# The order of the expert steps and the last scatter of a mixture-of-experts kernel

## The chip, the core and the metric

The kernel runs on one core of a Trainium2 chip. The core has a matmul engine (TensorE, PE in the profile; its weight loads are listed apart as PEld), a vector engine (VectorE, DVE), an engine for activations (ScalarE, ACT), a general one (GpSimd, POOL) and one that issues transfers (SyncE, SP), each with its own queue of instructions, and 16 DMA engines that move data between HBM and the on-chip memory. The metric is the device time of one execution in microseconds (us), the median of several; lower is better.

## The reference

Two layers of a diffusion backbone over 256 latent tokens and 256 context tokens with width 1024. Each layer mixes tokens by two kinds of gated recurrences and then channels; the first layer's channel mix is a dense SwiGLU, the second one's a mixture of eight experts, and only the latent tokens go through it. The change is about that last part and the final norm:

```python
logits = (t @ router).astype(jnp.float32)
top_v, top_i = lax.top_k(logits, TOP_K)                 # two of eight experts for each of 256 tokens
top_w = jax.nn.softmax(top_v, axis=-1)
gates = jnp.sum(jax.nn.one_hot(top_i, N_EXPERTS) * top_w[..., None], axis=1)
for e in range(N_EXPERTS):                              # w1, w3: 1024 x 3584, w2: 3584 x 1024, all float32
    y = y + gates[:, e:e + 1] * ((jax.nn.silu(t @ w1[e]) * (t @ w3[e])) @ w2[e])
x = x + m_lat[5] * y
return rmsnorm(x, final_norm_g)
```

## The kernel before, in words

Up to about 1000 us the kernel computes everything ahead of the experts; the change does not touch that. Then it routes the tokens: it counts how many go to each expert and sorts experts 1 to 7 by their count, so that from there on "expert r" is a rank (rank 0 is always expert 0). The ranks 1 to 4 have room for 128 tokens (`BIG`), the ranks 0, 5, 6 and 7 for 64 (`SMALL`); where an expert has more tokens than its room, code at the end of the kernel goes over them again, which the profiled execution did not enter.

The weights of an expert come as 42 tiles of 1 MB, and its work is cut into seven steps. A step (r, c) takes 512 columns of the hidden width: four tiles of w1 and w3 for the up product, two tiles of w2 for the down product. `steps` (line 182 on) lists the 56 steps of all experts in the order in which they run, the 128-slot ones in one sequence, the 64-slot ones in another, and `due` says how many of the 64-slot ones have to be placed by each position. The loop at line 1236 runs one turn for each step: the up product of step n (`up_big`, `up_small`), then the down product of step n-1 (`lower`), then the transposes of step n's hidden values (`turn_big`, `turn_small`), whose copy the down product of the next turn reads.

A 128-slot step computes in three products of two float32r halves: each half tile of weights is split into a high part by ScalarE (`wh`) and a low part by VectorE (`wl`), and TensorE multiplies wh by the tokens' high part, wl by the high part, and wh by the low part. A 64-slot step multiplies the float32 tiles as they are, two halves of the array side by side, and needs no split. The up product goes into the PSUM tiles `pj`, the down product of a 128-slot expert accumulates over its seven steps in two `po` tiles, that of a 64-slot expert in one `pj` tile, with rows 0 to 63 for the first 512 output columns and rows 64 to 127 for the others.

Three things sit beside the products. Before an expert's first step its tokens are gathered: `open_group` makes the one-hot matrix, `gather_group` multiplies by it in four pieces (with ScalarE and VectorE copying the results out), `back_group` transposes it for the way back. Two experts may share a gather (`members`): a 128-slot one and a 64-slot one. After an expert's last step `close` weighs the sum with the modulation, and `scatter` splits it (`halves`) and spreads it back over the tokens (`spill`: two matmuls and one VectorE sum into `x2t` for each half of the columns and each half of the tokens). For a 128-slot expert this is one scatter for each half of the columns, in two successive turns; for a 64-slot one a single scatter. `rest` hands gathers and scatters to `lower`, which puts one of them behind every group of down matmuls. After the last step `finish_half` squares and sums the residual for one half of the columns and multiplies by the norm's gain, and `finish_out` scales and writes.

The order of the instructions on each engine is the order of the code here (`strict[0]`), so an instruction waits for all those ahead of it on its engine. SyncE's queue issues the tiles in the order of `plan`: the up tiles of step n, then the down tiles of step n-1. A tile goes into the next of 12 buffers, and its transfer is issued when the buffer is free: for a 64-slot step when TensorE has used it, for a 128-slot step when both of its halves are split. `taken_pieces` (line 1173) sets how far the issue and the splits run ahead of the product: up to six half tiles, but no more than three that are split.

Of the kernel before, what the change touches and what calls it, by code (L numbers as in the profile page):

```python
# [16 lines left out]
D, T, KT = 1024, 256, 8  # L17
W, R = 64, 4
NE, DE = 8, 3584
# [15 lines left out]
def body(ctx, tc, I, out, dbg=None):  # L35
    nc = tc.nc
# [145 lines left out]
    big = [(r, c) for r in BIG for c in range(7)]  # L182
    small = [(r, c) for r in SMALL for c in range(7)]
    steps = []
    total, lead, tail = len(small), 3, 4
    for i in range(7 * NE):
        due = i + 1 if i < lead else min(total, lead + (i + 1 - lead) * (total - lead) / (7 * NE - lead - tail))
        steps.append((small if total - len(small) < int(due) else big).pop(0))
    chosen = {}

# [733 lines left out]
    def onehot(pos, widths):  # L924
        P = sb(mp, [128, 2, 256], F32R, "P", 1)
        o = 0
        for i, w in enumerate(widths):
            iota = C_IOTA if w == 128 else C_IOTH
            DVE.tensor_tensor(P[:, :, o:o + 128], con[:, None, iota:iota + 128].to_broadcast([128, 2, 128]),
                              pos[i].to_broadcast([128, 2, 128]), op=ALU.is_equal)  # L930
            o += 128
        return P
# [11 lines left out]
    def big_tiles():  # L944
        return sb(mp, [128, KT, 128], F32R, "xgh", 2), sb(mp, [128, KT, 128], F32R, "xgl", 2)

    def small_tile():
        return sb(mp, [128, KT, 64], F32, "xgs", 2)
# [135 lines left out]
    def down_big(ws, c, aT, ys, mid=(), halfway=None):  # L1084
        mid = list(mid)
        order = [(f, i) for f in range(4) for i in range(2)]
        if halfway:
            order[5:7] = order[6:4:-1]
        for n, (f, i) in enumerate(order):
            wt = tuple(t[:, 512 * i:512 * i + 512] for t in ws(f))  # L1090
            mm3(ys[i], (aT[0][:, f], aT[1][:, f]), wt, c == 0 and f == 0, c == 6 and f == 3)
            if mid:
                mid.pop(0)()
            if halfway and n == 5:
                halfway()
        for f in mid:
            f()
# [36 lines left out]
        return lambda tt: gater[:, tt, r:r + 1]  # L1134

    def members(g):
        return [g] + ([g + 4] if 0 < g < 4 else [])

    def open_group(g):
        if len(members(g)) == 2:  # L1140
            hot[g] = onehot([posr[:, :, g:g + 1], posr[:, :, g + 4:g + 5]], [128, 64])
            xgs[g], xgs[g + 4] = big_tiles(), small_tile()
        else:
            hot[g] = onehot([posr[:, :, g:g + 1]], [128])
            xgs[g] = big_tiles()

    def gather_group(g, k):
        gather([xgs[r] for r in members(g)], k, hot[g])
# [24 lines left out]
    def taken_pieces(n):  # L1173
        first = taken[0]
        taken[0] += n

        def at(k):
            i = first + k
            while (len(emitted) <= i or len(emitted) <= i + LOOK and sum(len(x) == 2 for x in emitted[i + 1:]) < 3) \
                    and next(feeder, 0) is None:  # L1180
                pass
            return tuple(x[:, 0] for x in emitted[i])
        return at
# [3 lines left out]
    def at_step(table, n, f):  # L1187
        table.setdefault(n, []).append(f)
# [6 lines left out]
        at_step(after, 0, lambda h=h: ACT.activation(m5[:, 512 * h:512 * h + 512], rows5[h], AF.Copy))  # L1195
    n = -5
    for g in BIG:
        free = {2: (0,), 3: (1, 5), 4: (2,)}.get(g, ())
        n = max([n + 5] + [1 + steps.index((r, 6)) for r in free])
        assert all(n + (3 if g == 1 else 4) <= steps.index((r, 0)) for r in members(g)), (g, n)  # L1200
        at_step(early if n else before, n, lambda g=g: open_group(g))
        for k in range(0, KT, 2):
            at_step(mids, n + 1 + k // 4 if g == 1 else n + k // 2, lambda g=g, k=k: gather_group(g, k))
        at_step(mids, n + 4, lambda g=g: back_group(g))
    acc, jobs = {}, []

    def close_half(r, i):
        jobs.append((r, weigh(acc[r][i], [(every, i)]), [(every, i)]))
# [8 lines left out]
    def scatter():  # L1217
        if not jobs:
            return []
        r, t, cuts = jobs.pop(0)  # L1220
        y = halves(t)
        return [lambda rows=rows, i=i, tt=tt: spill(y, rows, back[r], gate_of(r), i, tt)
                for rows, i in cuts for tt in range(2)]

    def lower(r, c, aT, mid):
        if c == 0:
            acc[r] = [bank("po") for i in range(2)] if r in BIG else bank("pj")
        if r in BIG:
            down_big(taken_pieces(4), c, aT, acc[r], mid)
        else:  # L1230
            down_small(taken_pieces(4), c, aT, acc[r], mid)
        if c == 6:
            close(r)
# [19 lines left out]
    r, c, aT = prev  # L1253
    z = sb(raws, [128, 2, D], F32, "w")

    left = []

    def begin(i):
        if i == 0:
            tc.keep_in_program_order(nc.scalar.preload_act_table_set("abs_reciprocal_sqrt_and_small"))  # L1260
        close_half(r, i)
        left.extend(scatter())

    down_big(taken_pieces(4), c, aT, acc[r], (), lambda: begin(0))
    for i in range(2):
        while left:
            left.pop(0)()
        if i == 0:
            begin(1)
        finish_half(z, i)  # L1270
    finish_out(z)
    strict[0] = False
# [133 lines left out]
```

## Time and profile before

| | before |
|---|---|
| median of 3 runs | 1889.72 us (1889.15 to 1893.68) |
| profiled execution | 1886.93 us, of which the span of the program 1885.1 us |
| TensorE busy | 1825.1 us (97%) |
| VectorE busy | 1203.9 us (64%) |
| ScalarE busy | 947.7 us (50%) |
| moved by DMA | 495.1 MB, mean 263 GB/s |
| expert weights | 336 transfers of 1 MB |
| TensorE's granted clock, mean | 0.99 |

Times in the profile are in us from the first instruction. Every matmul, split and copy of this kernel is recorded with line 47, that of a helper, so the rows are told apart by the names of the tiles: `pj<-w,xgs` is an up matmul of a 64-slot step, `pj<-w,aT` a down matmul of one (each listed as two instructions), `pj<-wh,xgh` and its like an up matmul of a 128-slot step, `po<-wh,aTh` a down matmul of one, `pp<-con,a` the transposes, `pp<-P,htkh` a gather, `pp<-y,PTa` or `PTb` a scatter. The end of a matmul is modelled, so that of two successive ones the starts tell more than the durations. An idle time in brackets names what ended it.

### The profile page before, as it was taken

What the parts mean: (1) busy time and instruction counts of PE and PEld (TensorE: products, weight loads), DVE (VectorE), ACT (ScalarE), POOL (GpSimd) and SP (SyncE); (2) the same over time, 40 slices, a digit from 0 to 9 for tenths busy, and PEclk for the clock granted to TensorE, in tenths of its full rate; (3) what the DMA queues carried; (4) which work ended last, traced back from release to release, by engine and by line L of the source; (5) the groups of instructions that cost most, each with busy time, mean ns of one, the idle gap of its engine ahead of it and who ended that gap; (6) DMA issues with size and microseconds to landing.
All of it is one profiled execution on the core that took longest, in us unless ns stands there. A gap on an engine that the chain in (4) does not pass through costs nothing.

```text
span 1885.1 us, 30248 instructions
## 1 busy us (share of the span) xinstructions
PE 1825.1 (97%) x11901; PEld 1329.5 (71%) x11901; DVE 1203.9 (64%) x1923; ACT 947.7 (50%) x1506; POOL 49.4 (3%) x94
## 2 busy tenths in 40 slices
PE   6999999999999999999999999999999999999995
PEld 4887778988888888987884556565656566565574
DVE  5699985788875337566763556565565656566485
ACT  4757664532222235666663545454455545354464
POOL 0111010000000000110000000000000000000000
PEclk9999999999999999999999999999999999999998
DMA  9344212456774324311264999999999999999991
GB/s 359 110 161 136 90 47 90 157 201 216 262 268 148 106 79 140 110 50 68 78 255 186 421 422 421 421 422 421 421 420 421 421 421 421 421 420 422 421 412 41
DMA packets 76731, 495.10 MB, mean 263 GB/s; under 512 B 8448, under 2 KB 10752, under 8 KB 23072
## 3 DMA queue, kind: packets, MB, share of 16 engines
q1 hardware_dynamic: 76576, 493.03, 66.1%
q8 instruction: 97, 1.59, 0.4%
q14 instruction: 58, 0.48, 0.1%
HBM read 491.95 MB, written 1.05 MB: 262 GB/s over the span
## 4 chain that ended last, share of the span: by engine, by line
PE 77%; DMA 8%; DVE 6%; ACT 6%; issue 2%; SPq 0%; ACTq 0%; DVEq 0%
PE pj L47 61%; PE po L47 11%; DMA w<-in_mw 7%; PE pp L47 6%; DVE wl L47 1%; ACT wh L47 1%; ACT kpad L47 1%; DVE junk L47 1%; DMA wm<-in_wmod 1%; ACT ptd L47 1%; DMA xT<-in_xT 1%; DVE Q L47 0%; DVE nt L47 0%; ACT F L47 0%; DVE hl L47 0%
## 5 line engine op out<-in xcount | busy, mean ns | idle before, releaser
L47 DVE TENSOR_TENSOR wl<-w,wh 128x1024 fp32r<-128x1024 f32 (+1 forms) x501 | 598.5, 1214 | 225.2 <-ACT wh L47 213.0
L47 ACT ACTIVATE wh<-w 128x1024 fp32r<-128x1024 f32 (+1 forms) x501 | 518.0, 1048 | 347.0 <-PE pj L47 260.5
L47 PE MATMUL pj<-hh,wh 128*128 128x512 f32 (+1 forms) x992 | 349.3, 353 | 1.5 <-ACT hh L47 1.0
L47 PE MATMUL pj<-hh,wl 128*128 128x512 f32 (+1 forms) x992 | 347.8, 351 | 1.7 <-DVE wl L47 1.7
L47 PE MATMUL pj<-hl,wh 128*128 128x512 f32 (+1 forms) x992 | 348.7, 352 | 0.5 <-DVE hl L47 0.5
L47 PEld LDWEIGHTS pj<-hh,wh 128*128 128x128 f32 x992 | 186.5, 188 | 30.3 <-issue 3.4
L47 PEld LDWEIGHTS pj<-hl,wh 128*128 128x128 f32 x992 | 186.7, 188 | 27.6 <-issue 2.5
L47 PEld LDWEIGHTS pj<-hh,wl 128*128 128x128 f32 x992 | 186.6, 188 | 26.6 <-DVE wl L47 2.5
L47 PE MATMUL pj<-w,xgs 128*64 128x512 f32 x896 | 199.8, 599 | 0.0
L47 DVE SCALAR_TENSOR_TENSOR junk<-wm,cbc 128x1024 bf16<-128x1024 f32 x128 | 156.3, 1221 | 41.3 <-DMA wm<-in_wmod 39.8
L47 PE MATMUL pj<-wh,xgh 128*128 128x512 f32 x448 | 180.5, 403 | 0.0
L47 PE MATMUL pj<-wl,xgh 128*128 128x512 f32 x448 | 178.5, 399 | 0.2 <-DVE wl L47 0.2
L47 PE MATMUL pj<-wh,xgl 128*128 128x512 f32 x448 | 178.1, 398 | 0.0
L47 PEld LDWEIGHTS pj<-w,xgs 128*64 128x64 f32 x896 | 62.2, 138 | 117.6 <-issue 116.9
L47 ACT ACTIVATE a<-pj 128x256 f32<-128x256 f32 (+1 forms) x78 | 40.3, 517 | 187.6 <-PE pj L47 187.6
L47 DVE TENSOR_TENSOR a<-a,pj 128x256 f32<-128x256 f32 (+1 forms) x78 | 45.9, 590 | 137.7 <-PE pj L47 85.0
L47 PE MATMUL pj<-w,aT 128*64 128x512 f32 x448 | 106.2, 602 | 0.0
L47 PEld LDWEIGHTS pj<-wl,xgh 128*128 128x128 f32 x448 | 84.8, 189 | 20.6 <-DVE wl L47 1.4
L47 PEld LDWEIGHTS pj<-wh,xgl 128*128 128x128 f32 x448 | 84.8, 189 | 20.5
L47 PEld LDWEIGHTS pj<-wh,xgh 128*128 128x128 f32 x448 | 84.8, 189 | 19.3
L47 PE MATMUL po<-wh,aTh 128*128 128x512 f32 x224 | 94.1, 420 | 0.7 <-ACT aTh L47 0.7
L47 PE MATMUL po<-wl,aTh 128*128 128x512 f32 x224 | 89.8, 401 | 0.9 <-DVE wl L47 0.9
(273 smaller groups left out, 2442.1 us busy)
## 6 DMA issues: line engine op xcount, KB each, us to landing
w<-in_mw SPq DMA_DIRECT2D x336, 1024.0 KB, 18.5
wm<-in_wmod SPq DMA_DIRECT2D x80, 512.0 KB, 4.1
w<-in_win SPq DMA_DIRECT2D x31, 1024.0 KB, 4.8
w<-in_fw SPq DMA_DIRECT2D x30, 1024.0 KB, 4.9
w<-in_wout SPq DMA_DIRECT2D x12, 1024.0 KB, 4.8
wg<-in_wgroup SPq DMA_DIRECT2D x8, 1024.0 KB, 14.2
w<-in_fw SPq DMA_DIRECT2D x8, 768.0 KB, 4.3
xT<-in_ctxT SPq DMA_DIRECT2D x1, 1024.0 KB, 8.0
```

Of the source, the lines that this page charges most:

```text
L47: ins = fn(*args, **kw)
```

## The change

It has three parts. The list of steps begins with four 64-slot steps instead of three and ends with three 64-slot steps behind the spread-out part instead of four steps of 128 slots; with B for a 128-slot step and s for a 64-slot one the two orders are

```
before  sssBsBsBsBsBsBsBsBsBsBsBsBsBsBsBsBsBsBsBsBsBsBsBsBssBBBB
now     ssssBBsBsBsBBsBsBsBBsBsBsBBsBsBsBBsBsBsBBsBsBsBBsBsBssss
```

Since the 64-slot experts come later, rank 7 shares its gather with rank 4 instead of rank 3, and the pieces of a gather are placed by the turn in which the group is first needed. And because the last step is now of a 64-slot expert, the last scatter is one split with four spreads, with `finish_half` for a half of the columns behind the two spreads that complete it; the code that closed the first half of a 128-slot expert in the middle of its last down product is no longer called.

```diff
--- before.py
+++ after.py
@@ -182,9 +182,10 @@
     big = [(r, c) for r in BIG for c in range(7)]
     small = [(r, c) for r in SMALL for c in range(7)]
     steps = []
-    total, lead, tail = len(small), 3, 4
+    total, lead, tail = len(small), 4, 3
     for i in range(7 * NE):
-        due = i + 1 if i < lead else min(total, lead + (i + 1 - lead) * (total - lead) / (7 * NE - lead - tail))
+        mid = (i + 1 - lead) * (total - lead - tail) / (7 * NE - lead - tail)
+        due = i + 1 if i < lead else lead + mid if i < 7 * NE - tail else total - (7 * NE - 1 - i)
         steps.append((small if total - len(small) < int(due) else big).pop(0))
     chosen = {}
 
@@ -1134,12 +1135,13 @@
         return lambda tt: gater[:, tt, r:r + 1]
 
     def members(g):
-        return [g] + ([g + 4] if 0 < g < 4 else [])
+        return [g] + {1: [5], 2: [6], 4: [7]}.get(g, [])
 
     def open_group(g):
         if len(members(g)) == 2:
-            hot[g] = onehot([posr[:, :, g:g + 1], posr[:, :, g + 4:g + 5]], [128, 64])
-            xgs[g], xgs[g + 4] = big_tiles(), small_tile()
+            o = members(g)[1]
+            hot[g] = onehot([posr[:, :, g:g + 1], posr[:, :, o:o + 1]], [128, 64])
+            xgs[g], xgs[o] = big_tiles(), small_tile()
         else:
             hot[g] = onehot([posr[:, :, g:g + 1]], [128])
             xgs[g] = big_tiles()
@@ -1195,12 +1197,15 @@
         at_step(after, 0, lambda h=h: ACT.activation(m5[:, 512 * h:512 * h + 512], rows5[h], AF.Copy))
     n = -5
     for g in BIG:
-        free = {2: (0,), 3: (1, 5), 4: (2,)}.get(g, ())
+        free = {2: (0,), 3: (1,), 4: (2, 5)}.get(g, ())
         n = max([n + 5] + [1 + steps.index((r, 6)) for r in free])
-        assert all(n + (3 if g == 1 else 4) <= steps.index((r, 0)) for r in members(g)), (g, n)
+        first = min(steps.index((r, 0)) for r in members(g))
+        per = 2 if n + 4 <= first and g > 1 else 4
+        done = (n + 1 if g == 1 else n) + KT // per
+        assert done <= first, (g, n)
         at_step(early if n else before, n, lambda g=g: open_group(g))
         for k in range(0, KT, 2):
-            at_step(mids, n + 1 + k // 4 if g == 1 else n + k // 2, lambda g=g, k=k: gather_group(g, k))
+            at_step(mids, done - KT // per + k // per, lambda g=g, k=k: gather_group(g, k))
         at_step(mids, n + 4, lambda g=g: back_group(g))
     acc, jobs = {}, []
 
@@ -1253,20 +1258,12 @@
     r, c, aT = prev
     z = sb(raws, [128, 2, D], F32, "w")
 
-    left = []
-
-    def begin(i):
-        if i == 0:
-            tc.keep_in_program_order(nc.scalar.preload_act_table_set("abs_reciprocal_sqrt_and_small"))
-        close_half(r, i)
-        left.extend(scatter())
-
-    down_big(taken_pieces(4), c, aT, acc[r], (), lambda: begin(0))
+    tc.keep_in_program_order(nc.scalar.preload_act_table_set("abs_reciprocal_sqrt_and_small"))
+    lower(r, c, aT, ())
+    left = scatter()
     for i in range(2):
-        while left:
-            left.pop(0)()
-        if i == 0:
-            begin(1)
+        for f in left[2 * i:2 * i + 2]:
+            f()
         finish_half(z, i)
     finish_out(z)
     strict[0] = False
```

VectorE ahead of the first 128-slot step, before (`wl` is the low part of a weight split, `a` the hidden values of a step, `xgl` the low part of gathered tokens; the numbers are those of buffers, which differ between the two programs):

```order
L47 TENSOR_TENSOR a_10510<-a_10510,pj_10485 128x256
L47 TENSOR_TENSOR xgl_10471<-g_10527,xgh_10470 128x256
L47 TENSOR_TENSOR xgl_10471<-g_10545,xgh_10470 128x256
L47 TENSOR_TENSOR wl_10585<-w_10582,wh_10584 128x1024
L47 TENSOR_TENSOR wl_10591<-w_10582,wh_10590 128x1024
L47 TENSOR_TENSOR a_10596<-a_10596,pj_10563 128x256
L47 TENSOR_TENSOR wl_10602<-w_10599,wh_10601 128x1024
L47 TENSOR_TENSOR xgl_10471<-g_10616,xgh_10470 128x256
L47 TENSOR_TENSOR xgl_10471<-g_10634,xgh_10470 128x256
L47 TENSOR_TENSOR wl_10653<-w_10599,wh_10652 128x1024
```

The same place now:

```order
L47 TENSOR_TENSOR a_10510<-a_10510,pj_10485 128x256
L47 TENSOR_TENSOR xgl_10471<-g_10527,xgh_10470 128x256
L47 TENSOR_TENSOR xgl_10471<-g_10545,xgh_10470 128x256
L47 TENSOR_TENSOR a_10588<-a_10588,pj_10563 128x256
L47 TENSOR_TENSOR xgl_10471<-g_10604,xgh_10470 128x256
L47 TENSOR_TENSOR xgl_10471<-g_10622,xgh_10470 128x256
L47 TENSOR_TENSOR wl_10662<-w_10659,wh_10661 128x1024
L47 TENSOR_TENSOR wl_10668<-w_10659,wh_10667 128x1024
L47 TENSOR_TENSOR a_10673<-a_10673,pj_10640 128x256
L47 TENSOR_TENSOR wl_10679<-w_10676,wh_10678 128x1024
```

The product `a` of the step ahead of the first 128-slot one stands behind two splits as before, one step later in the plan; the last two gather copies, which stood behind three splits, now have none ahead of them.

VectorE at the end of the program, before, from the last split on (`a<-po` weighs, `y` is the low part of the scatter's split, `x2t` the sums of the scatter, `w<-x2t` the product with the norm's gain, `fr` the sum of squares):

```order
L47 TENSOR_TENSOR wl_16256<-w_16233,wh_16255 128x1024
L47 TENSOR_TENSOR a_16278<-po_15192,m_9881 128x512
L47 TENSOR_TENSOR y_16280<-a_16278,y_16280 128x512
L47 SCALAR_TENSOR_TENSOR x2t<-pp_16289,gater,x2t 128x512
L47 SCALAR_TENSOR_TENSOR x2t<-pp_16293,gater,x2t 128x512
L47 TENSOR_TENSOR a_16297<-po_15193,m_9881 128x512
L47 TENSOR_TENSOR y_16299<-a_16297,y_16299 128x512
L47 TENSOR_TENSOR w_16254<-x2t,xgh_15546 128x512 x2
L47 SCALAR_TENSOR_TENSOR x2t<-pp_16308,gater,x2t 128x512
L47 SCALAR_TENSOR_TENSOR x2t<-pp_16312,gater,x2t 128x512
L47 TENSOR_TENSOR w_16254<-x2t,xgh_15546 128x512 x2
L47 TENSOR_TENSOR fr<-fs 128x2
```

And now, from the weighing of the last expert on:

```order
L47 TENSOR_TENSOR a_16260<-a_16260,pj_16235 128x256
L47 TENSOR_TENSOR a_16288<-pj_15498,m_9881 64x512 x2
L47 TENSOR_TENSOR y_16291<-a_16288,y_16291 128x512
L47 SCALAR_TENSOR_TENSOR x2t<-pp_16294,gater,x2t 128x512
L47 SCALAR_TENSOR_TENSOR x2t<-pp_16298,gater,x2t 128x512
L47 TENSOR_TENSOR w_16278<-x2t,xgh_15849 128x512 x2
L47 SCALAR_TENSOR_TENSOR x2t<-pp_16308,gater,x2t 128x512
L47 SCALAR_TENSOR_TENSOR x2t<-pp_16312,gater,x2t 128x512
L47 TENSOR_TENSOR w_16278<-x2t,xgh_15849 128x512 x2
L47 TENSOR_TENSOR fr<-fs 128x2
```

The two weighings are of 64 rows each and stand together, with one split for both halves of the columns; the sums and products behind them are in the same order as before.

TensorE at the end, before, from the last down matmuls on:

```order
L47 MATMUL po_15193<-wh_16235,aTl_16251 128x512
L47 MATMUL po_15193<-wh_16255,aTh_16250 128x512
L47 MATMUL po_15193<-wl_16256,aTh_16250 128x512
L47 MATMUL po_15193<-wh_16255,aTl_16251 128x512
L47 MATMUL pp_16289<-y_16280,PTa_14007 128x512 x2
L47 MATMUL pp_16293<-y_16280,PTa_14007 128x512 x2
L47 MATMUL pp_16308<-y_16299,PTa_14007 128x512 x2
L47 MATMUL pp_16312<-y_16299,PTa_14007 128x512 x2
```

And now:

```order
L47 MATMUL pp_16273<-con,a_16260 128x128 x2
L47 MATMUL pj_15498<-w_16254,aT_16276 64x512 x4
L47 MATMUL pj_15498<-w_16263,aT_16276 64x512 x4
L47 MATMUL pp_16294<-y_16291,PTb_14013 128x512 x2
L47 MATMUL pp_16298<-y_16291,PTb_14013 128x512 x2
L47 MATMUL pp_16308<-y_16291,PTb_14013 128x512 x2
L47 MATMUL pp_16312<-y_16291,PTb_14013 128x512 x2
```

The last down product is eight matmuls of a 64-slot step, and the four spreads follow it without a weighing between them.

## Rows read from the trace of the kernel before

**Rows 1.** The page's part 2: what the DMA engines moved in 40 slices.
```profile
GB/s 359 110 161 136 90 47 90 157 201 216 262 268 148 106 79 140 110 50 68 78 255 186 421 422 421 421 422 421 421 420 421 421 421 421 421 420 422 421 412 41
```

**Rows 2.** What SyncE's queue waited for, 1036 to 1140 us: total, times, longest.
```profile
SPq L47 <- DMA w<-in_mw: 82.5, 41, 2.1
```

**Rows 3.** The same, 1500 to 1780 us.
```profile
SPq L47 <- PE pj L47: 93.4, 51, 5.8
...
SPq L47 <- DMA w<-in_mw: 46.4, 33, 2.4
```

**Rows 4.** Timeline: start, length, engine, operation; TensorE at starts of steps, two of ScalarE.
```profile
1182.74 1.51 PE L47 MATMUL pj<-w,xgs 128*64 128x512 f32 x6
...
1190.17 1.06 ACT L47 ACTIVATE wh<-w 128x1024 fp32r<-128x1024 f32 x1 [0.49 <-DMA w<-in_mw]
...
1203.90 0.48 PE L47 MATMUL pj<-wh,xgh 128*128 128x512 f32 x1
...
1220.70 0.65 PE L47 MATMUL pj<-w,xgs 128*64 128x512 f32 x2
...
1263.66 0.47 PE L47 MATMUL pj<-wh,xgh 128*128 128x512 f32 x1
...
1280.94 0.65 PE L47 MATMUL pj<-w,xgs 128*64 128x512 f32 x2
...
1610.72 0.65 PE L47 MATMUL pj<-w,xgs 128*64 128x512 f32 x2
...
1627.00 0.48 PE L47 MATMUL pj<-wh,xgh 128*128 128x512 f32 x1
...
1642.59 0.65 PE L47 MATMUL pj<-w,xgs 128*64 128x512 f32 x2
...
1655.47 0.47 PE L47 MATMUL pj<-wh,xgh 128*128 128x512 f32 x1
...
1671.06 0.65 PE L47 MATMUL pj<-w,xgs 128*64 128x512 f32 x2
...
1772.12 0.65 PE L47 MATMUL pj<-w,xgs 128*64 128x512 f32 x2
...
1784.01 0.44 PE L47 MATMUL pp<-con,a 128*128 128x128 f32 x2 [1.38 <-DVE a L47]
...
1784.55 0.39 ACT L47 ACTIVATE aT<-pp 128x256 f32<-128x256 f32 x1 [0.83 <-PE pp L47]
...
1838.12 0.48 PE L47 MATMUL pj<-wh,xgh 128*128 128x512 f32 x1
```

**Rows 5.** Windows: length, busy PE, PEld, DVE, ACT, POOL, clock, DMA share, GB/s.
```profile
1655.47:1671.06 15.59, 15.59 (x72) 10.42 (x70) 7.70 (x7) 6.18 (x7) 0.00 (x0) 1.00 1.02 421
1820.80:1838.12 17.32, 17.32 (x80) 13.96 (x78) 15.71 (x15) 13.49 (x14) 0.00 (x0) 1.00 0.95 396
```

**Rows 6.** Windows, after the last tile.
```profile
1842.00:1844.00 2.00, 2.00 (x10) 1.63 (x9) 1.81 (x3) 1.33 (x2) 0.00 (x0) 1.00 0.00 0
```

**Rows 7.** Timeline: a 64-slot down product, the last down matmul, the sum of squares.
```profile
1061.48 3.65 PE L47 MATMUL pj<-w,aT 128*64 128x512 f32 x16
...
1862.11 0.39 PE L47 MATMUL po<-wh,aTl 128*128 128x512 f32 x1
...
1871.20 0.15 DVE L47 TENSOR_TENSOR fr<-fs 128x2 f32<-128x2 f32 x1
```

**Rows 8.** Timeline ahead of the first 128-slot step.
```profile
1043.42 2.00 ACT L47 ACTIVATE wh<-w 128x1024 fp32r<-128x1024 f32 x2 [11.34 <-DMA w<-in_mw]
...
1046.79 0.41 DVE L47 TENSOR_TENSOR a<-a,pj 128x256 f32<-128x256 f32 x1
...
1048.35 0.44 PE L47 MATMUL pp<-con,a 128*128 128x128 f32 x2 [3.69 <-DVE wl L47]
```

**Rows 9.** Windows with a lower clock.
```profile
1048.50:1052.00 3.50, 3.50 (x11) 2.73 (x11) 0.85 (x2) 2.94 (x9) 0.00 (x0) 0.53 1.01 421
1195.50:1202.00 6.50, 6.50 (x19) 4.62 (x20) 3.45 (x4) 1.77 (x4) 0.00 (x0) 0.50 1.01 416
```

## The prediction, made before the changed kernel ran

> **What bounds the kernel now.** I read the page's slices first, then who waits for whom, then the order of time around the first and the last expert steps, since the change touches nothing ahead of 1018 us. From there to the last two the slices stand at 420 to 422 GB/s [rows 1], which looks like a kernel that waits for its weights. The queue that issues the transfers says otherwise. Early in the expert stage SyncE waits for earlier transfers, 82.5 us of 104 [rows 2]; between 1500 and 1780 us it waits for them only 46.4 us of 280, and 93.4 us for a tile that TensorE has yet to free [rows 3]. The transfers run ahead, and TensorE holds their buffers.
>
> TensorE's own rows bear this out. A cycle is the time from one step's first matmul to the next one's: the up product of the new step, the down product of the step before, the transposes between. A 64-slot up behind a 128-slot step costs 12.88 us (1642.59 to 1655.47), a 128-slot up behind a 64-slot step 15.59 (1655.47 to 1671.06), two 64-slot steps 10.51 up to the next transposes (1772.12 to 1784.01, less the 1.38 of waiting) [rows 4]. Two 128-slot steps in a row cost 17.32, the stretch from the first matmul of the last step but one to that of the last, in which TensorE is busy throughout [rows 5]. A step's six tiles of 1.049 MB need 6 x 2.49 = 14.94 us at 421 GB/s. An alternating pair takes TensorE 28.47 us and the transfers 29.88; what TensorE has to do besides (gathers, scatters) fills the difference and more. Both are nearly full, TensorE slightly fuller: no tile lands after 1842 us [rows 6], and TensorE's last down matmul ends at 1862.50 [rows 7], 20 us later.
>
> The Trainium skill ("Perfetto Trace Analysis", section "Identifying the Most-Contended Engine") would have TensorE's headroom judged by its weight loads and the transfers by HBM utilization; by that page's table of peaks 421 GB/s is 118% of a core's share, while the weight loads fill 67% of an alternating cycle here [rows 5], so by the rule the transfers bind and the first rival's time below would come out. The trace disagrees in the later part, where the issuing queue waits for buffers [rows 3].
>
> **The change, part by part.** First, the start. Before the first 128-slot step TensorE waits 3.69 us for the transposes at 1048.35: the product they need stands on VectorE behind two weight splits, and these wait for a tile that lands at 1043.42 and for the one 2.49 later [rows 8]. With a fourth small step in front, the tiles of the first 128-slot step come six tiles, 14.94 us, later in the plan: 1058.4 and 1060.9. The two ScalarE splits behind the first take until 1060.5, VectorE's until 1061.9, the product 0.41: the transposes come free at about 1062.3. In the rows of before they come 1.15 us after the product ends, behind gather evacuations caught in the same queue; in the new order no split stands ahead of these, so I leave this out, and keep 1063.3 as the upper end. After its wait TensorE ran at a granted clock of 0.53 for 3.5 us [rows 9]; this is inside the sum of before, and I let it stand once in the new one.
>
> Second, the middle. From 1048.35 to the last step's first matmul at 1838.12 [rows 4, 8] are 789.8 us in 52 cycles: 25 of a 128-slot up behind a 64-slot step, 24 the other way, two of two large, one of two small, 389.8 + 309.1 + 34.6 + 10.5 = 744.0 us; the other 45.8 are gathers, scatters, stalls. The new order has 51 cycles there: 21, 21, seven, two, or 327.4 + 270.5 + 121.2 + 21.0 = 740.1 us. Of the 45.8 two items go. The cycle at 1182.74 takes 21.16 us, 8.28 over its price, though its parts are a 64-slot scatter (3.40: 1610.72 to 1627.00 is 16.28 against 12.88) and one gather (1.21: 1203.90 to 1220.70 is 16.80 against 15.59): 3.7 us are a pile-up, in which ScalarE waits for a tile at 1190.17 [rows 4] and TensorE runs at half clock for 6.5 us [rows 9]. In the new order this scatter and this gather fall on two 128-slot steps in a row, and the tiles next in the plan are a 64-slot step's, which have no split to block VectorE's queue; I let the 3.7 go. The other is the 1.38 us ahead of the transposes at 1784.01, where TensorE had caught up with the transfers. The last expert's scatter leaves this stretch and that of expert 4 enters it: 3.40 out, two halves of 1.69 in (1263.66 to 1280.94 is 17.28 against 15.59 [rows 4]), nothing in sum. That leaves 40.7. The last step starts at 1062.3 + 740.1 + 40.7 = 1843.1, 5.0 us later than before.
>
> Third, the end. Before, from the last step's first matmul to the end of its last down matmul are 1862.50 - 1838.12 = 24.4 us. Now a 64-slot up and down follow: 10.5 to the transposes, 0.9 to the end of the copy behind them (1784.01 to 1784.94 [rows 4]), 3.65 for the down product [rows 7], 15.1 us: 1858.2, that is 4.3 us earlier. The tiles are there by then. The first of the four closing steps starts 12.9 + 2 x 10.5 + 2 x 1.7 us ahead of the last one, at 1806; at full rate its first tile lands 25 tiles before the last, at 1842 - 62 = 1780, so all twelve buffers are held. Of the 26 tiles from it on, 14 to 16 have yet to land, 40 us at the most, and TensorE needs 52 for them.
>
> Fourth, the last scatter. Behind the last down matmul VectorE had, in order, `y`, two sums, `a`, `y`, two products, two sums, two products: 11 instructions, and the end of the chain at 1871.20, 8.7 us after [rows 7]. Now it has two `a`, one `y` and the same eight: 11 again, each on 512 columns. One wait for ScalarE goes, and the first half's sums are no longer begun under the down product's end. I take nothing in sum, 0.7 us either way. The activation table is loaded under the last down product, where ScalarE has nothing else.
>
> The sum is 4.3 us less on the profiled execution of 1886.9 us: 1882.6. The median of the runs shown is 2.8 above that execution: 1885.4. About 5.7 us (0.3%) is the least that a measurement of this kernel tells from no change. The unknown costs: the start 1.0 later, or 1.5 earlier without the half clock; the rest of the stalls inside the 40.7 gone, some 2 less; one more pile-up, 3.7 more. That is 1882 to 1890 for this case.
>
> **Rivals.** *The transfers are the bound.* Then the end follows the last tile: 1842 us and 1.8 for the half of the down product that it feeds, 1843.8 in place of 1862.5, 18.7 less: 1871. For it: 421 GB/s in every slice, and TensorE's waits at both ends of the stage stem from tiles [rows 4, 8]. Against it: the 740 us of prices are TensorE's work without a wait in it, and a new order sheds none of it. This is the gain that shows if the end is looked at alone.
>
> *Pile-ups of scatter and gather.* The new order brings the two together in six cycles (12, 16, 17, 28, 29 and 30, counted from 0); before it was four (12, 26, 31, 32), and one of them cost 3.7 us beyond its parts. One of the six has large steps on both sides, where VectorE is busy 15.71 of 17.32 us without them [rows 5]. From the third that pays, the result is over the bound: -4.3 + 3 x 3.7 = +6.8; with four, +10.5: 1900. Against it: the other three of before paid nothing, with TensorE further behind the transfers, as it will be here.
>
> *The start costs what the end gives.* If the later first large step brings a second stretch at half clock (another 1.5) and the upper end of its wait (1.0), and one pile-up stays (3.7), the sum is +1.9: 1892. Every part of that is seen in before.
>
> **How the numbers follow.** The forecast's case gets 0.65, the transfers 0.07, pile-ups from three on 0.12, the start with one pile-up 0.16. The forecast's spread of 1882 to 1890 has the bound of 1884.05 inside its lower third, so 0.26 of its 0.65 is faster; with the transfers' case 0.33. Slower are the pile-ups, 0.12. The rest, 0.55, is no change that can be measured. The range of 1880 to 1894 leaves out the transfers' case, most of the pile-ups and a little on the low side.
>
> **What would show it.** The transposes ahead of the first 128-slot step at 1062 to 1063.5 us; the last step's first matmul at 1840 to 1846; the end of its last down matmul some 15 us later; then 8.7 us to the end of the chain. The transfers should fall below 421 GB/s somewhere in the last 150 us before the closing steps, because TensorE holds all twelve buffers; before, they did so only at the end. The cycle of the first scatter should take 17.3 + 4.6 us and no more. I am wrong on the main point if TensorE waits for tiles in the last four steps, or if its cycles no longer come at these prices.

## The result, and the profile after

The changed kernel takes 1881.31 us (median of 5 runs, 1878.13 to 1883.87), the kernel before 1889.72 beside it: a ratio of 0.995, with a 95% interval of 0.9933 to 0.9967. It is faster by 0.5%, beyond the 0.3% that a measurement tells from no change. The forecast was 1885.4 us, 4.3 us off the path; the path lost more.

To compare executions I count from the first matmul of the expert stage, because that stage began at anything from 1006.92 to 1014.18 us in the 13 profiles of this study, although the change touches nothing ahead of it. In the profile of before it is at 1008.33 us and the last down matmul ends at 1862.49, 854.16 later; after, 1010.61 and 1858.43, 847.82 later. That is 6.34 us less. Then 8.46 us to the sum of squares where it was 8.70.

The first view is the page's slices of GB/s, 40 of them, which answer to [rows 1].

```profile
GB/s 360 104 164 128 102 47 89 158 190 222 238 268 178 90 94 141 91 69 68 68 231 185 421 421 421 421 421 421 421 421 420 396 400 419 421 420 414 405 422 153
```

From slice 32 on the transfers fall to 396 and 400, again to 405 near the end: every buffer is taken, and a transfer waits until one comes free. What SyncE's queue waited for between 1500 and 1780 us says the same (total, times, longest), against [rows 3]:

```profile
SPq L47 <- DVE wl L47: 121.2, 54, 4.9
SPq L47 <- PE pj L47: 95.7, 45, 5.4
SPq L47 <- DVE a L47: 1.9, 6, 0.3
```

The 46.4 us of waiting for earlier transfers are gone; every wait is for a buffer. And TensorE, from its first 128-slot step to the last transposes, shows no wait for another engine at all.

The timeline (start, length, engine, operation, idle time before it) ahead of the first 128-slot step, where [rows 8] had the transposes at 1048.35 with 3.69 us of waiting:

```profile
1053.46 1.94 PE L47 MATMUL pj<-w,xgs 128*64 128x512 f32 x8 [0.53 <-DMA w<-in_mw]
1056.04 1.94 PE L47 MATMUL pj<-w,aT 128*64 128x512 f32 x8 [0.64 <-DMA w<-in_mw]
1058.43 1.94 PE L47 MATMUL pj<-w,aT 128*64 128x512 f32 x8 [0.46 <-DMA w<-in_mw]
1064.74 0.69 PE L47 MATMUL pp<-con,a 128*128 128x128 f32 x2 [4.36 <-DVE a L47]
```

The turn of the fourth 64-slot step itself waits for three tiles, and the long wait stands where it stood, one step later. The last step and the tail, against the end of [rows 4] and [rows 7]:

```profile
1843.35 3.22 PE L47 MATMUL pj<-w,xgs 128*64 128x512 f32 x14
...
1854.78 3.65 PE L47 MATMUL pj<-w,aT 128*64 128x512 f32 x16 [0.53 <-ACT aT L47]
1858.48 1.39 DVE L47 TENSOR_TENSOR a<-pj,m 64x512 f32<-64x512 f32 x2 [7.15 <-PE pj L47]
...
1861.85 1.41 DVE L47 SCALAR_TENSOR_TENSOR x2t<-pp,gater,x2t 128x512 f32<-128x512 f32 x2 [0.59 <-PE pp L47]
...
1863.17 1.29 DVE L47 TENSOR_TENSOR w<-x2t,xgh 128x512 f32<-128x512 f32 x2
...
1864.37 1.41 DVE L47 SCALAR_TENSOR_TENSOR x2t<-pp,gater,x2t 128x512 f32<-128x512 f32 x2
...
1865.69 1.28 DVE L47 TENSOR_TENSOR w<-x2t,xgh 128x512 f32<-128x512 f32 x2
...
1866.89 0.16 DVE L47 TENSOR_TENSOR fr<-fs 128x2 f32<-128x2 f32 x1
```

15.08 us from the last step's start to the end of its down product, where before had 24.4; behind it VectorE's instructions follow each other without a gap from 1861.85. Three windows of this kernel (length, busy PE, PEld, DVE, ACT, POOL, clock, DMA share, GB/s): the cycle of the first scatter, which shares its turn with a gather, the stretch behind the wait at the start, and two us behind the last tile.

```profile
1186.42:1208.19 21.77, 21.77 (x95) 15.71 (x94) 16.77 (x19) 12.41 (x17) 0.00 (x0) 1.00 1.01 420
...
1064.75:1068.25 3.50, 3.50 (x10) 2.87 (x11) 2.29 (x2) 1.56 (x3) 0.00 (x0) 0.56 1.01 419
1851.50:1853.50 2.00, 2.00 (x12) 0.57 (x8) 0.00 (x0) 0.00 (x0) 0.00 (x0) 1.00 0.00 0
```

The scatter's cycle is TensorE's work alone, at full clock. The half clock at the start stands once, as before. The last tile is there by 1851.5, though TensorE's last product that needs it begins only at 1854.78 and reaches it 5.2 us after it landed.

### The profile page after: what moved, and what is told of

The parts are those of the page before. It is cut to its first block, busy times and chain, and to the rows that moved or that the text cites. A ratio compares the mean times of both kernels' runs of the same rounds, so it can differ in the third digit from the quotient of the medians.

```text
span 1881.9 us, 30271 instructions
## 1 busy us (share of the span) xinstructions
PE 1821.9 (97%) x11901; PEld 1330.4 (71%) x11901; DVE 1206.6 (64%) x1923; ACT 947.1 (50%) x1506; POOL 49.4 (3%) x94
## 5 line engine op out<-in xcount | busy, mean ns | idle before, releaser
L47 DVE TENSOR_TENSOR a<-a,pj 128x512 f32<-128x512 f32 (+1 forms) x78 | 46.0, 590 | 135.4 <-ACT a L47 80.3
L47 ACT ACTIVATE a<-pj 128x512 f32<-128x512 f32 (+1 forms) x78 | 40.2, 516 | 178.3 <-PE pj L47 178.2
L47 PE MATMUL po<-wh,aTl 128*128 128x512 f32 x224 | 88.8, 396 | 0.0
## 6 DMA issues: line engine op xcount, KB each, us to landing
w<-in_mw SPq DMA_DIRECT2D x336, 1024.0 KB, 12.8
```

What stands on the lines that cost most here:

```text
L47: ins = fn(*args, **kw)
```

## The experiments

All device times below are medians beside runs of before on the same chip; "the path" is the time from the first expert matmul to the end of the last down matmul in the profiled execution.

**What sets the end, before and after.** In the next two kernels the second w2 tile of the steps 20 to 35 is not loaded; the first is used in its place, so the products are the same in number and the values are not. 16 transfers of 2.49 us, 40 us, are left out. The edit is the same in the changed kernel and in the one before:

```diff
+    last = [None]
...
-        w = chunk(src() if callable(src) else src, a, b)
+        if src == "again":
+            w = last[0]
+        else:
+            w = last[0] = chunk(src() if callable(src) else src, a, b)
...
+            if 20 <= i - 1 < 36:
+                plan[-1] = ("again",) + plan[-1][1:]
```

In the changed kernel:

> The changed kernel with the second tile of the down weights left out in steps 20 to 35: the step uses its first tile twice, so 16 of 336 transfers (40 us at 2.49) are not made, with all splits and matmuls as they were. If TensorE sets the time from the first 128-slot step to the end, nothing moves: 847.8 us from the first expert matmul to the last down matmul's end, within 1 us. If the transfers set it, up to 40 us less.

Measured: 1881.82 us, path 847.73 against 847.82. The tiles do not set the changed kernel's time; since TensorE waits for no engine from the first 128-slot step on, its own work does.

In the kernel before:

> The kernel before with the same 16 transfers left out. By TensorE's ledger only the waits at 1782 to 1784 us go, 1.5 us: 852.7 us from the first expert matmul to the last down matmul's end in place of 854.2. If the transfers set the time up to the four closing steps, up to 40 us less.

Measured: 1882.76 us, a ratio to before of 0.9968 (0.9954 to 0.9982), path 849.46: 4.7 us less than before. That is three times what I had expected from TensorE's work and a tenth of what the transfers' rival wanted. SyncE's queue between 1500 and 1780 us, against [rows 3], and the window where [rows 9] had a clock of 0.50 (the stage began 1.75 us later):

```profile
SPq L47 <- PE pj L47: 111.9, 57, 7.5
SPq L47 <- DVE wl L47: 105.7, 46, 4.9
```

```profile
1197.20:1203.70 6.50, 6.50 (x33) 4.84 (x32) 4.35 (x7) 3.97 (x9) 0.00 (x0) 1.00 1.01 413
```

With the tiles early, the waits for transfers go, and so does the wait of [rows 4] at 1784; the stretch at half clock is not there either, although the kernel is the same as before up to this point. That leaves a doubt: 2.95 of the 4.7 us lie in the cycle of that stretch and 0.7 at the start, ahead of the first tile left out. The cycle took 21.16 us in before and takes 18.21 here:

```profile
1184.64:1202.85 18.21, 17.32 (x75) 8.67 (x75) 12.56 (x16) 9.69 (x15) 0.00 (x0) 1.00 1.01 418
```

The next two runs remove it. They have all their tiles and no half clock in that cycle, and still their paths are 855.24 and 854.04; the last tile lands 833.8 and 833.7 us after the first expert matmul, 833.8 in before. So in before both sides had a hand: TensorE at full clock had work for 849.5 us, and the tiles kept it until 854 either way.

**Is the pile-up of before worth its 3.7 us?** One line puts the gather of rank 2 two steps later, off the step of the first scatter:

```diff
         n = max([n + 5] + [1 + steps.index((r, 6)) for r in free])
+        n = 13 if g == 2 else n
```

> The kernel before, with the gather of ranks 2 and 6 opened two steps later (steps 13 to 16 in place of 11 to 14), so that the first 64-slot scatter meets no more than its own step. The cycle of 21.15 us should fall to about 16.3 (12.88 and 3.40) and TensorE keep its full clock there. By the ledger of the prediction, in which this pile-up of 3.7 us counts in full, the end comes 3.7 us earlier: 850.5 us from the first expert matmul to the last down matmul's end in place of 854.2. The rival: TensorE had caught up with the transfers by 1784 us, so what is won at 1200 is waited for there, the 1.38 us of waiting becoming about 5, and the end moves by less than 0.5 us.

Measured: 1889.24 us, ratio 1.0002 (0.9992 to 1.0011), path 855.24. Windows of the cycle, of the stretch that had half clock in before and of one near the end; ScalarE's wait in the cycle and TensorE's longest near the end; SyncE's for transfers, 1500 to 1780 us.

```profile
1183.34:1201.85 18.51, 16.67 (x68) 7.78 (x67) 12.48 (x16) 8.70 (x10) 0.00 (x0) 1.00 1.01 420
...
1197.20:1203.70 6.50, 6.50 (x28) 4.77 (x28) 5.69 (x8) 3.62 (x5) 0.00 (x0) 1.00 1.02 417
1787.20:1790.60 3.40, 3.40 (x10) 2.63 (x9) 2.45 (x2) 1.70 (x3) 0.00 (x0) 0.50 1.01 422
```

```profile
1189.57 2.00 ACT L47 ACTIVATE wh<-w 128x1024 fp32r<-128x1024 f32 x2 [4.64 <-DMA w<-in_mw]
...
1785.75 0.44 PE L47 MATMUL pp<-con,a 128*128 128x128 f32 x2 [2.71 <-DVE a L47]
```

```profile
SPq L47 <- DMA w<-in_mw: 85.1, 56, 2.3
```

The cycle took 18.51 us instead of 21.16, more than the theory's 16.3: without the gather, ScalarE's splits wait for tiles there, and TensorE 1.8 us for splits and sums. And nothing came of it: TensorE met the tiles again at 1785, waited 2.71 us ahead of the transposes instead of 1.38, and the half clock came behind that wait. The rival had the reason right, but the end moved by 1.1 us, later, where it had said less than 0.5. SyncE's queue waited 85.1 us for transfers, not 46.4. What is won early in before is handed back near the end.

**The longer start alone.**

```diff
-    total, lead, tail = len(small), 3, 4
+    total, lead, tail = len(small), 4, 4
```

> The kernel before with four 64-slot steps at the front and its old ending (a lone 128-slot step spread-out part, then four 128-slot steps). All times here count from the first expert matmul to the end of the last down matmul; before 854.16 us, after 847.82. Theory: before's end is set by the tiles, which TensorE catches up with at the last 64-slot steps, four 128-slot steps from the end; a longer start changes nothing there, so 853 to 855.5 and a device time within 1.5 us of before. Rival (only TensorE's own work counts, and the new start is a part of the gain): the same steps in the same pairs, about 1.5 us more at the start, no wait at the catch-up: 849.5 to 851.5, some 4 us faster than before. Second rival (the start is a pure cost): 856 to 858.

Measured: 1887.9 us, ratio 0.9994 (0.9983 to 1.0004), path 854.04. The theory's case: no gain, and no loss either, since the end waits for tiles. Its queue waits for transfers longest of all (1500 to 1780 us):

```profile
SPq L47 <- DMA w<-in_mw: 162.0, 95, 2.6
```

**The new ending with the old start.** In the changed kernel:

```diff
-    total, lead, tail = len(small), 4, 3
+    total, lead, tail = len(small), 3, 3
```

> The changed kernel with three 64-slot steps in front instead of four; the end stays as changed. If TensorE's work sets the time (each step at its price, the transfers ahead), the first 128-slot step comes 14.1 us earlier with 10.7 us less done, so the wait ahead of it is 3.4 us shorter and the end is 3.4 us earlier than in the changed kernel: from the first expert matmul to the end of the last down matmul 844.4 us in place of 847.8, unless TensorE then reaches the last tiles (it was 5.2 us behind them). If the transfers set the time, their last tile lands when it did, and the kernel is within 0.5 us of the changed one. If the new order makes scatter and gather pile up, 3.7 us later than the first figure.

Measured: 1883.16 us, ratio 0.9968 (0.9958 to 0.9979), path 849.61. All of the change but the longer start brings 4.6 us of the gain by itself. The shorter start did not bring its 3.4 on top; it lost 1.8, later than all three figures expected. The loss is in three cycles, 13 to 15 (with the half clock inside the third), and in the third TensorE waited twice:

```profile
1199.04:1217.06 18.02, 18.02 (x88) 12.18 (x86) 9.22 (x12) 9.59 (x17) 0.00 (x0) 1.00 1.01 422
1217.06:1235.11 18.05, 18.05 (x83) 9.56 (x83) 13.20 (x16) 9.92 (x17) 0.00 (x0) 1.00 1.01 421
1235.11:1256.18 21.07, 19.53 (x75) 11.81 (x74) 11.49 (x13) 8.31 (x13) 0.00 (x0) 0.92 1.01 421
...
1242.80:1246.20 3.40, 3.40 (x10) 2.63 (x9) 3.40 (x4) 1.65 (x2) 0.00 (x0) 0.50 1.02 424
```

```profile
1240.60 0.50 PE L47 MATMUL pj<-wh,xgh 128*128 128x512 f32 x1 [0.78 <-ACT wh L47]
...
1241.86 0.50 PE L47 MATMUL pj<-wl,xgh 128*128 128x512 f32 x1 [0.76 <-DVE wl L47]
```

The gather must be done by step 15, so it goes two pieces to a turn, beside the scatter; VectorE's sums and copies stand ahead of the splits, the 128-slot step behind them finds its splits late, and half clock follows the waits. The prices of the pairs are 15.59, 12.88 and 15.59: 13.1 us over.

**Gather and scatter apart.** The same steps, but rank 2 gathered alone in steps 6 to 9:

```diff
-        return [g] + {1: [5], 2: [6], 4: [7]}.get(g, [])
+        return [g] + {1: [5], 3: [6], 4: [7]}.get(g, [])
...
-        free = {2: (0,), 3: (1,), 4: (2, 5)}.get(g, ())
-        n = max([n + 5] + [1 + steps.index((r, 6)) for r in free])
+        free = {3: (0, 1), 4: (2, 5)}.get(g, ())
+        n = max([n + 5, {2: 6, 3: 18, 4: 32}.get(g, 0)] + [1 + steps.index((r, 6)) for r in free])
...
-        at_step(mids, n + 4, lambda g=g: back_group(g))
+        at_step(mids, 16 if g == 2 else n + 4, lambda g=g: back_group(g))
```

> Three 64-slot steps at the front and three behind the spread-out part, as in the run with lead 3 and tail 3, but rank 2 is gathered alone in steps 6 to 9, and rank 6 shares the gather of rank 3, so that no gather meets a scatter. In that run the steps 13 to 21 took 19.1 us more than the prices of their pairs, in the changed kernel the like stretch (12 to 19) 14.1, and the end came at 849.61 us from the first expert matmul. Theory (the scatter and the gather met there and piled up): the pile-ups of some 5 us go, and about 1 us at steps 28 to 30: 843.5 to 845.5, a device time of 1877 to 1880. Rival (the 128-slot pairs that follow each other at the front cost this, not the gather): 849 to 850.5, as with lead 3 and tail 3. Second rival (the tiles set the end as soon as TensorE is earlier): 847 to 849, with waits for tiles in the closing steps.

Measured: 1877.19 us, ratio 0.9942 (0.9923 to 0.9961), path 844.50. The theory's number. The same three cycles, 13 to 15:

```profile
1203.16:1218.75 15.59, 15.59 (x71) 10.42 (x69) 8.17 (x8) 6.18 (x7) 0.00 (x0) 1.00 1.01 421
1218.75:1235.03 16.28, 16.28 (x68) 7.79 (x67) 12.66 (x16) 8.58 (x10) 0.00 (x0) 1.00 1.01 421
1235.03:1252.33 17.30, 17.30 (x76) 10.75 (x74) 10.82 (x12) 6.42 (x8) 0.00 (x0) 1.00 1.01 420
```

They take 5.1 us over the prices, the parts of one scatter (3.40) and one half of the next (1.7); the gather costs 4.0 in steps 6 to 10. That is 9.1 us where the shared gather with lead 3 had 13.1; 1.0 more is won at steps 28 to 36. (The 19.1 us in the expectation are those of steps 13 to 22; 13 to 21 make 18.6.)

That run changed two things, the place of the gather and its density. So once more, with two pieces to a turn, still apart (`g > 1` becomes `g > 2` where `per` is set):

> As the run with the gathers apart (844.50 us from the first expert matmul to the last down matmul, 1877.19 us), but the gather of rank 2 goes two pieces to a turn, in steps 6 and 7 instead of 6 to 9, as it did in the run with lead 3 and tail 3 (849.61 us). Theory (the pile-up there came from the gather and the scatter in the same turns): the packed gather alone costs no more than the one spread out, some 4.2 us over the prices of steps 6 to 10, and the end stays at 844 to 845.3. Rival (two pieces in a turn are what blocks VectorE's queue): steps 6 to 9 cost 7 us or more over their prices, with TensorE waiting for a split, and the end comes at 847 to 850.

Measured: 1878.9 us, path 845.29. The first three cycles of this gather:

```profile
1098.50:1116.47 17.97, 17.97 (x88) 12.18 (x86) 8.88 (x10) 8.63 (x13) 0.00 (x0) 1.00 1.01 421
1116.47:1131.12 14.65, 14.65 (x76) 8.71 (x75) 8.35 (x17) 9.91 (x16) 0.00 (x0) 1.00 1.01 422
1131.12:1147.44 16.32, 15.84 (x72) 10.41 (x70) 9.62 (x9) 8.77 (x10) 0.00 (x0) 1.00 1.01 420
```

4.9 us over the prices of 15.59, 12.88 and 15.59, 4.7 with the two cycles behind them: 0.7 more than spread out, and no difference in device time to the spread-out version on the same chip (1878.94, below). So density alone is not what cost four; the place is, beside the scatter in the two turns right ahead of the step that needs the result. Whether a gather in these turns would cost as much without a scatter, no run shows.

**The last scatter.** All four spreads first, the norm of both halves behind them:

```diff
+    for f in left:
+        f()
     for i in range(2):
-        for f in left[2 * i:2 * i + 2]:
-            f()
         finish_half(z, i)
```

> The changed kernel with all four spreads of the last scatter first and the norm of both column halves behind them. From the end of the last down matmul to the sum of squares after takes 8.46 us. Theory: VectorE's eleven instructions behind the last down matmul set this stretch, whatever their order, so 8.2 to 8.9 us and a device time within 1.5 us of after (1880 to 1883). Rival: the norm behind each half is a gain of its own, because the squares of the first half run on ScalarE while VectorE sums the second; then two squares of 0.8 us each come later, 9.8 to 10.1 us, and the device time is 1.4 us more.

Measured: 1881.71 us, path 847.79, and 9.21 us to the sum of squares: between the two expectations for this stretch, so both missed; the device time is the theory's. VectorE's rows:

```profile
1865.39 1.41 DVE L47 SCALAR_TENSOR_TENSOR x2t<-pp,gater,x2t 128x512 f32<-128x512 f32 x2 [0.59 <-PE pp L47]
...
1866.99 0.75 DVE L47 SCALAR_TENSOR_TENSOR x2t<-pp,gater,x2t 128x512 f32<-128x512 f32 x1 [0.19 <-PE pp L47]
...
1868.11 0.75 DVE L47 SCALAR_TENSOR_TENSOR x2t<-pp,gater,x2t 128x512 f32<-128x512 f32 x1 [0.37 <-PE pp L47]
...
1868.78 2.48 DVE L47 TENSOR_TENSOR w<-x2t,xgh 128x512 f32<-128x512 f32 x4
...
1871.18 0.15 DVE L47 TENSOR_TENSOR fr<-fs 128x2 f32<-128x2 f32 x1
```

It is VectorE's sequence still, not the squares (ScalarE is done at 1869.68), but now it waits 0.56 us for spreads that the products of the first half used to cover. The same instructions in the other kernels of this ending took 8.46 or 8.85 to 8.95 us, so 0.3 to 0.75 us is what the interleaving is worth; the device time does not show it.

**How many closing steps?** In the changed kernel `lead, tail` is `4, 5`:

> The changed kernel with five 64-slot steps instead of three behind the spread-out part. It has two more pairs of 128-slot steps and two more of 64-slot steps, by their prices 1.3 us less of TensorE's work: 846.5 us from the first expert matmul to the last down matmul if TensorE alone sets the time (after 847.82). Theory: six closing 64-slot steps use up the buffers' lead. The changed kernel used its last tile 5.2 us after it landed, and each closing step loses 2.5 to 4.4 us of that; two steps more leave TensorE waiting 0 to 3.6 us for tiles at the end: 847 to 850. Rival (the closing steps go at their price however many): 846 to 847, no wait.

Measured: 1881.8 us, path 849.10. The number falls into the theory's range for another reason than the theory's. TensorE waits for no tile in the closing steps, and the last one landed 1.0 us ahead of its use. The loss lies at the front. The half clock behind the start lasts 6.8 us instead of 3.4, which costs 1.3, and the steps 12 to 20 are 16.0 us over their prices, 14.3 in the changed kernel: the packed gather meets the first scatter in cycles 12 and 13. Cycles 12 to 14:

```profile
1186.27:1204.29 18.02, 18.02 (x88) 12.17 (x86) 9.21 (x12) 9.60 (x17) 0.00 (x0) 1.00 1.01 419
1204.29:1222.34 18.05, 18.05 (x84) 9.57 (x83) 13.21 (x17) 9.92 (x17) 0.00 (x0) 1.00 1.01 422
1222.34:1238.01 15.67, 15.67 (x72) 10.33 (x70) 11.63 (x11) 10.74 (x15) 0.00 (x0) 1.00 1.02 421
```

The first two read like those with lead 3, but here a 128-slot step of the old expert lies between the gather and the step that needs it. TensorE waits for no split, the third cycle takes 15.67 us where it took 21.07, and the meeting costs 1.7 us at the most where it cost four. Beside the changed kernel's second profile (below, 848.80), whose start also had 6.8 us of half clock, the path is 0.3 longer. That six closing 64-slot steps nearly use up the lead of the buffers (1.0 us is left where the changed kernel has 5.2) is shown; that a seventh would wait is not.

**The changed kernel and the version with gathers apart, side by side on one chip.**

> The changed kernel once more, unaltered, beside the version with the gathers apart. If its gain over before is what its path shows (6.3 us less from the first expert matmul to the last down matmul), 847.5 to 848.2 us there and a device time 5 to 8 us below before. The version with the gathers apart should stand 3.3 us lower by its path, 2.5 to 5 by device time. Rival (device times of this kernel are too uneven for that): the two medians overlap within 1.5 us.

> The version with the gathers apart once more, beside the changed kernel on the same chip: 844 to 845 us from the first expert matmul to the last down matmul, a device time 2.5 to 5 us below the changed kernel's, 9 to 13 below before. Rival: no more than 1.5 us below the changed kernel.

Measured: the changed kernel 1881.76 us (ratio 0.9948, 0.9933 to 0.9962; path 848.80), the other 1878.94 (0.9934, 0.992 to 0.9949; path 844.48). The changed kernel is 9.2 us below before, more than the 5 to 8 expected, and its path is longer than the 847.5 to 848.2; the other's figures are as expected. The path repeats to 0.02 us for the second and is 1.0 longer for the first, whose start ran at half clock for 6.8 us instead of 3.4. The two medians are 2.8 us apart, the runs overlap (1878.82 to 1883.53 and 1876.79 to 1882.14), as do the intervals: the version with gathers apart is faster on its path, by 3.3 to 4.3 us, and probably in device time.

## Why the prediction was right, and where not

**The start**: right. The transposes were forecast for 1062.3 us; they came at 1064.74, and 1062.46 when the later beginning of the stage, 2.28 us, is taken off.

**The middle**: the prices held to 0.01 us (the 64-slot cycles at 12.88, the 128-slot ones behind them at 15.59), and the first scatter's cycle took 21.77 for the forecast 17.3 + 4.6; only two 64-slot steps in a row came 0.3 over their 10.51 at the end. From the transposes to the last step 778.6 us passed, against 740.1 + 40.7 = 780.8. The step that failed is the 40.7, the stalls taken over from before: it should have been 38.5. Two of before's 64-slot cycles, with nothing scattered or gathered in them, were over their price by 1.12 and 0.46 us, since TensorE was 4 to 5 us behind the tiles there; here they are, and then one of the changed kernel, where it is 9 us behind:

```profile
1123.02:1137.02 14.00, 13.33 (x60) 6.84 (x59) 7.38 (x8) 9.00 (x10) 0.00 (x0) 1.00 1.01 421
...
1152.61:1165.95 13.34, 13.15 (x60) 6.92 (x59) 7.48 (x8) 7.42 (x9) 0.00 (x0) 1.00 1.01 421
```

```profile
1099.97:1112.85 12.88, 12.88 (x59) 6.92 (x59) 8.63 (x9) 8.18 (x9) 0.00 (x0) 1.00 1.01 419
```

That makes 1.6 of the 2.2 us, which the prediction had named as stalls that might go, and had not taken. The other 0.6 is what is left of larger differences both ways around the gathers and scatters; they are not traced further.

**The end**: right. Last step 1841.1 (1843.35 less 2.28) for 1843.1, 15.08 us for 15.1, the tail 8.46 for 8.7, the transfers under 421 GB/s in the later part.

**What bounds before**: wrong in part, and it is why the change pays. I read that TensorE was slightly fuller than the transfers and put the tiles' part at the 1.38 us of waiting at 1784. The run without 16 tiles puts it at 4.7: the wait is short because TensorE arrives there at a time that the tiles set, whatever happened ahead. The gathers moved, the start lengthened, and the path stayed at 854 to 855. For the same reason the 3.7 us "let go" at 1182.74 were no gain. Nor were they what a gather costs a scatter: with both in one cycle as before, but at full clock, the cycle is 5.34 us over its price in the run without 16 tiles and 4.76 in the one with the longer start, against 4.61 for the parts. The rest of before's 8.28 was the half clock, which the other profiles of the old order do not have there. The sum survived this because all but its 40.7 was built from TensorE's prices in the new order, where no tile is late behind the start. Of the 6.34 us, then, 4.7 are the tiles that no longer set the end (4.0 without the 0.7 at the start of that run), and 1.6 are TensorE's, changed kernel against the old order without the 16 tiles: 2.7 less by the prices (four more pairs of two large steps, three more of two small ones, a small step's down product at the end), 3.3 less for gathers, scatters and stalls from step 5 on, 4.3 more for the start.

How does the change get rid of that wait? The old order kept four 128-slot steps, 17.3 us each for 14.94 us of tiles, for the end, where the last tiles come in and their slowness helps nobody; the new one spreads such pairs through the stage and ends with steps that need less TensorE time than tile time. The trace has it in how far a step starts behind the landing of its first tile: in before 4.1 us at the first of the four closing steps and 13.3 at the last, a lead that nothing uses; now 23.6 us at step 48 (counted from 0) and 9.3 at the last. The Trainium skill ("Perfetto Trace Analysis", section "Optimization Strategy") says of kernels with several regimes that interleaving them can help; the runs here agree: the new order with the old start brought 4.6 us, the new start with the old ending 0.1.

**The rivals.** The transfers as the bound (1871) fell for the changed kernel: 40 us fewer of them moved its path by 0.09 us. So the rule that had spoken for it, the Trainium skill's "Identifying the Most-Contended Engine" in the same page, does not name the bound of the changed kernel: its transfers run at 421 GB/s through most of the stage, over the page's peak for a core, and are not the bound. Pile-ups did not come: the cycles 12 to 15 are 7.0 us over their prices, one scatter (3.4) and a gather's parts, and the other five of the six cycles named are 2.2 to 4.0 over. They are real, though: with three steps at the start, or with five at the end, the gather is packed into the scatter's turns; where the next step needs its result, that cost 4 us. The start with one pile-up did not come either.

**The size.** 1881.31 us lies 0.7 below the forecast case's 1882 to 1890, inside the wider range. The forecast took the path's change, -4.3, and the offset of before's profiled execution to the median, +2.8. The path gave -6.3, the tail -0.24, and the medians differ by 8.4, with an interval of 6.2 to 12.7 us. The offset was luck of that one execution, the fastest of before on its chip (1886.93 against 1889.15 to 1893.68); with after it is the other way about, the profiled run was the slowest of five (1883.87). The chances leant to "no change" because a gain of 4.3 lies inside what can be told and one of 6.6 does not. Whether the last 1 to 2 us of the medians are the stage's beginning or waits that before has in other executions stays open.

## What to carry to other kernels

Where two resources are nearly balanced, a short wait late in the stage is not its price: leave out some of the other resource's work, keep the rest, and see what the path does. Build the time of a new order from the work in it, pair by pair, rather than from what the old one loses. Steps that are slow on the engine and light on transfers belong where transfers still have something to catch up on, not at the end. And work that can be placed freely, as a gather can, belongs some turns ahead of the step that needs it, the more so where a scatter stands in the same turns.

## What the runs showed of the hardware beside that

- The granted clock is not the same from one execution to the next: the stretch of 6.8 us at half speed at 1195.5 us in before is in none of the other three profiles of the old order, while the one behind the long wait at the start is in 12 of the 13 profiles, for 3.4 us (granted 0.50) in nine and 6.8 in three. The same program, the changed kernel, had 3.4 in one profile and 6.8 in another.
- The path from first expert matmul to last down matmul repeats well (847.82, 847.73 and 847.79 us for three profiles of the same expert steps, 844.50 and 844.48 for two), and one profile of the changed kernel is 1.0 longer by its clock at the start. The device time of the same kernel spreads over 3 to 10 us between its runs; in the profiles, the stage begins at 1006.9 to 1014.2 us and the output takes 12.8 to 15.1 us behind the sum of squares.
